# The head of an expert search: one half of the tokens first, and a shorter search for its first eight rows

## The chip, the cores and the metric

The kernel runs on one core of a Trainium2 chip. The metric is the device time of one execution in microseconds (us); less is better. The core has TensorE (PE), VectorE (DVE), ScalarE (ACT), GpSimd (POOL) and SyncE (SP, which here only issues DMAs), and 16 DMA engines that serve all queues.

## The reference, cut to what matters

Three model blocks run one after the other over 256 tokens of 1024 channels. The change lies where the second block ends and its expert layer (PEER) begins:

```python
def peer(h, wq, subkeys, u_tab, v_tab):
    q = (hf @ wq).reshape(T, PEER_HEADS, 2, PEER_DKEY // 2)          # 8 heads, two halves of 128
    sc = jnp.einsum('thpd,pnd->thpn', q, subkeys)                    # two lists of 128 scores
    top_v, top_i = lax.top_k(sc, PEER_TOPK)                          # 16 best of each list
    cand_v = top_v[:, :, 0, :, None] + top_v[:, :, 1, None, :]       # 256 sums of a pair
    best_v, best_j = lax.top_k(cand_v, PEER_TOPK)                    # the 16 best pairs
    ids = jnp.take_along_axis(cand_id, best_j, axis=-1)              # 16 rows of a table of 16384
    ...
```

`h` is the RMS-normed, modulated residual stream. Each token and head takes 16 rows `u`, `v` of the table; the layer's result is the sum over `gate * gelu(h . u) * v`. So 256 tokens x 8 heads x 16 rows are gathered.

## The kernel before

**Weights.** All weights come through one ring of five 512 KB slots: `_load` issues them on SP in a fixed order, each as soon as its slot is free. `_process` splits the next one into a high part (ACT, line 111) and a low part (DVE, line 115; GpSimd if asked); the slot is free when the low part is done. Three pairs of parts (`SPLIT`) can be held. `get` hands out the next pair and works ahead up to three. Each product is three matmuls (`mm3`: high x high, high x low, low x high). Every engine works off its instructions in the order in which the program writes them.

**End of the second block.** `x_add(g, r, p)` takes a product of 512 channels, scales it on DVE (line 976), adds it to `x` for each half `t` of the tokens (line 979; DVE for `g = 1, t = 1`, else GpSimd) and squares the result on ACT with a sum per token (line 237). `later` puts a call off, `settle` writes the calls that were put off.

**Head of `peer`.** The root of the sums of squares is taken for both halves at once (`rms_x`), both halves of `x` are scaled into `xn` (line 1071), the first two weights of `wq` are split (`ahead`, the second one's low part on GpSimd), and 16 transposes with their evictions give `hT` for 256 tokens. While TensorE has nothing to do, `keep_warm` writes idle transposes (line 278). Then, for head `r` = 0 and 1: `pair` makes the head's 48 matmuls of 256 columns, `half_scores` copies them to `q3` (line 1077), `half_products` multiplies by the subkeys (line 1084) and copies the scores to `sc` (line 1087), and `pump(99, r)` writes the whole search of the first 128 tokens for that head to DVE.

**The search** (`choose`) of one set `s` (128 tokens, one head) has 13 steps: the 8 best of 128, the next 8, for two lists (`top8`), 256 sums, the 16 best of them, and a decoding into row numbers `ids[s]` (line 1133) and gates. The table's rows are then gathered by GpSimd (line 1180), one indirect DMA per row `n` (128 tokens x 8 KB); set `s` is rows 16 s to 16 s + 15. Twelve places of 1 MB hold rows at first. `choice(n)` makes the dot product with row `n` (DVE, line 1206), the gate (ACT, lines 1215 to 1218) and the weighted sum (TensorE, line 1222), which frees the row's place. Beside the rows, every fourth `n` one more weight of `wq` is split and multiplied, and from `n = 16` one step of the search of set 2 is written behind most dots, so that the last step stands behind the dot of row 29.

Of the kernel before, what the change touches and what calls it, by code (L numbers as in the profile page):

```python
# [821 lines left out]
def block2(k, mod, M):  # L822
    nc, tc, a, x = k.nc, k.tc, k.a, k.x
# [21 lines left out]
    st = {}  # L845
# [184 lines left out]
def peer(k, mod, pA, normed_at):  # L1030
# [3 lines left out]
    nc, tc, a, x = k.nc, k.tc, k.a, k.x  # L1034
    tk = tc.alloc_tile_pool(name="tk", bufs=1, reuse_waits="tile")
# [4 lines left out]
    iota16 = tk.tile([128, 16], F32, name="iota16")  # L1040
# [22 lines left out]
    def halves(z):  # L1063
        return z.rearrange("p (s e) -> p s e", s=2)
# [1 line left out]
    topv, topi = [small(64 * i) for i in range(2)], [small(64 * i + 32, 32, U32) for i in range(2)]  # L1066
    bestv, besti = [small(128 + 32 * i, 16) for i in range(2)], [small(144 + 32 * i, 16, U32) for i in range(2)]
    topf, ji, jf, sel = small(192), small(224, 32, U32), small(256), small(288)
    r = k.rms_x(tk, "m2")
    for t in range(2):  # L1070
        nc.vector.tensor_scalar_mul(xn[:, t], x[:, t], r[:, t:t + 1])
    k.ahead(2)
    k.transposed(hT, xn, normed_at[0], normed_at[1], tmp=hfull, warm=40)
    nc.scalar.dma_start(subk, a["subk"])

    def half_scores(r, p):
        nc.scalar.activation(q3, p, AF.Copy)
        k.later(half_products, r)

    def half_products(r):  # L1080
        q, ps = q3, k.mm()
        for n in range(2):
            for t in range(2):
                nc.tensor.matmul(ps[:, t * 256 + n * 128:t * 256 + n * 128 + 128], q[:, n, t * 128:t * 128 + 128],
                                 subk[:, n * 128:n * 128 + 128], start=True, stop=True)
        for t in range(2):
            nc.scalar.activation(sc[t][:, 2 * r:2 * r + 2], ps[:, t * 256:t * 256 + 256], AF.Copy)

# [4 lines left out]
    def top8(v, i, src, n):  # L1093
        nc.vector.max(out=v[:, 8 * n:8 * n + 8], in_=src)
        nc.vector.max_index(out=i[:, 8 * n:8 * n + 8], in_max=v[:, 8 * n:8 * n + 8], in_values=src)
        if n == 0:
            nc.vector.match_replace(out=src, in_to_replace=v[:, 0:8], in_values=src, imm_value=-3.0e38)

    def choose(s):
        t, h = s // 8, s % 8  # L1100
        tv, ti, bv, bi = (z[s % 2] for z in (topv, topi, bestv, besti))
        st = {}

        def sums():
            nc.vector.tensor_tensor(cand.rearrange("p (a b) -> p a b", a=16),
                                    tv[:, 0:16].unsqueeze(2).to_broadcast([128, 16, 16]),
                                    tv[:, 16:32].unsqueeze(1).to_broadcast([128, 16, 16]), op=ALU.add)

        def gate():
            st["g"] = tk.tile([128, 16], F32, name="gate", bufs=6)  # L1110
            st["z"] = tk.tile([128, 2], F32, name="gz", bufs=2)
            nc.vector.tensor_scalar_mul(st["z"][:, 0:1], bv[:, 0:1], -1.0)
            nc.scalar.activation(st["g"], bv, AF.Exp, bias=st["z"][:, 0:1], accum_out=st["z"][:, 1:2])

        def decode():
            nc.vector.tensor_copy(topf, ti)
            nc.vector.tensor_scalar(ji[:, 0:16], bi, 4, None, op0=ALU.logical_shift_right)
            nc.vector.tensor_scalar(ji[:, 16:32], bi, 15, None, op0=ALU.bitwise_and)
            nc.vector.tensor_copy(jf, ji)

        def equal():
            nc.vector.tensor_tensor(eq, halves(jf).unsqueeze(3).to_broadcast([128, 2, 16, 16]),
                                    iota16.unsqueeze(1).unsqueeze(1).to_broadcast([128, 2, 16, 16]), op=ALU.is_equal)

        def pick():
            nc.vector.tensor_mul(eq, eq, halves(topf).unsqueeze(2).to_broadcast([128, 2, 16, 16]))

        def total():
            nc.vector.reduce_sum(halves(sel), eq, axis=AX.X)

        def rows():
            ids[s] = tk.tile([128, 16], I32, name="ids", bufs=6)
            nc.vector.scalar_tensor_tensor(ids[s], sel[:, 0:16], 128.0, sel[:, 16:32], op0=ALU.mult, op1=ALU.add)
# [6 lines left out]
        z = [lambda i=i, n=n: top8(tv[:, 16 * i:16 * i + 16], ti[:, 16 * i:16 * i + 16], sc[t][:, 2 * h + i], n)  # L1140
             for i in range(2) for n in range(2)]
# [26 lines left out]
    st = {"n": 0}  # L1168

    def refill():  # L1170
        while places and st["n"] < N and st["n"] // 16 in ids:
# [7 lines left out]
            i = ids[n // 16]  # L1179
            nc.gpsimd.indirect_dma_start(out=z, out_offset=None, in_=a["uv"],  # L1180
                                         in_offset=bass.IndirectOffsetOnAxis(ap=i[:, n % 16:n % 16 + 1], axis=0))
            st["n"] += 1

    def release(n):
# [8 lines left out]
    def tokens(t):  # L1193

        h2[0] = ps.tile([128, 1024], F32, name="h2")
        for c in range(8):
            nc.tensor.transpose(h2[0][:, c * 128:c * 128 + 128], hfull[:, c, t * 128:t * 128 + 128], k.ident)
# [56 lines left out]
    def rest():  # L1254
        for r in range(2, 8):
# [1074 lines left out]
```

## Time and profile before

| what | value |
| --- | --- |
| median of the runs (3) | 2525.92 us (2523.03 to 2526.9) |
| the profiled execution | 2522.51 us, its span 2520.6 us |
| granted TensorE clock, mean | 0.913 of full |
| DMA | 861.29 MB, mean 342 GB/s |
| busy: PE, DVE, ACT, POOL | 81%, 51%, 30%, 13% |

The profile is of one execution. The busy share of a span is a mean over stages with different limits: the stage that matters here runs from about 618 us (last products of the second block) over 669 us (first gather issued) to about 1380 us (last row used). "Idle before" in a row is the time that the engine stood still ahead of it, with the instruction that ended the wait.

### The profile page before, as it was taken

The page shows a single profiled execution, that of the slowest core. Times are in us where ns is not written, and L with a number is a line of the kernel's source. Part 1 is how long each engine was busy: PE and PEld are TensorE (multiplying, and loading weights), DVE is VectorE, ACT ScalarE, POOL GpSimd, SP SyncE. Part 2 cuts the span into 40 slices and gives each one's busy share as a digit, 9 for nine tenths or more (in the row PEclk, how much of TensorE's full clock was granted, in tenths as well). Part 3 has the DMA queues.
Part 4 walks back from the last instruction along what each step waited for, and adds up shares of the span by engine and source line. Part 5 has one row for each costly group of instructions (what it writes and reads, how often), then busy time and mean ns, then how long its engine had stood idle before and what let it go on. Part 6 is the DMA issues. An engine that isn't in the chain of part 4 may idle for free. (4 is left out here: it accounts for less than half of the span.)

```text
span 2520.6 us, 30184 instructions
## 1 busy us (share of the span) xinstructions
PE 2051.9 (81%) x11204; PEld 1195.5 (47%) x11204; DVE 1297.8 (51%) x2518; ACT 766.4 (30%) x1637; POOL 327.8 (13%) x315
## 2 busy tenths in 40 slices
PE   9899999899699888787886898966776676676766
PEld 8789898787555333343432897321221111121121
DVE  8987799877767687787855888100000000000001
ACT  5654444446344444454543443000000000000000
POOL 0100000000334333333341121000000000000000
PEclk9999999999899989899999999988778888888887
DMA  7767688775599999999998448999999999999997
GB/s 263 236 216 256 202 313 300 251 252 173 201 420 397 421 417 369 355 400 393 381 417 352 117 149 319 378 418 419 418 418 419 418 418 419 417 417 419 417 417 289
DMA packets 176307, 861.29 MB, mean 342 GB/s; under 512 B 29992, under 2 KB 35296, under 8 KB 107296
## 3 DMA queue, kind: packets, MB, share of 16 engines
q1 hardware_dynamic: 125872, 578.19, 59.9%
q0 software_dynamic: 36864, 268.45, 26.4%
q10 hardware_dynamic: 13424, 12.72, 1.7%
q8 instruction: 89, 1.46, 0.2%
q14 instruction: 58, 0.48, 0.1%
HBM read 858.19 MB, written 1.10 MB: 341 GB/s over the span
## 5 line engine op out<-in xcount | busy, mean ns | idle before, releaser
L115 DVE TENSOR_TENSOR wlo<-ring,whi 128x1024 fp32r<-128x1024 f32 x223 | 276.1, 1242 | 96.6 <-ACT whi L111 93.9
L1972 DVE TENSOR_TENSOR xe<-mm,m 128x256 f32<-128x256 f32 x15 | 6.4, 424 | 602.0 <-PE mm L1970 602.0
L111 ACT ACTIVATE whi<-ring 128x1024 fp32r<-128x1024 f32 x228 | 239.6, 1056 | 163.1 <-PE mm L162 40.3
L2014 PE MATMUL mm<-K,xe 128*32 128x512 f32 x864 | 147.1, 654 | 84.8 <-DMA K<-in_moe_w_dram 84.5
L2014 PE MATMUL mm<-we,xe 128*32 128x512 f32 x864 | 145.3, 765 | 84.1 <-DMA we<-in_moe_w_dram 83.7
L1222 PE MATMUL ys<-rowsS,diag 128*128 128x512 f32 x264 | 143.8, 685 | 53.6 <-ACT diag L1218 53.4
L161 PE MATMUL mm<-hTh,whi 128*128 128x256 f32 x608 | 172.4, 284 | 0.8 <-DVE hTl L309 0.8
L163 PE MATMUL mm<-hTh,wlo 128*128 128x256 f32 x608 | 169.6, 279 | 0.4 <-DVE wlo L115 0.4
L162 PE MATMUL mm<-hTl,whi 128*128 128x256 f32 x608 | 169.5, 279 | 0.0
L2035 ACT ACTIVATE he<-mm 128x512 f32<-128x512 f32 x16 | 9.5, 597 | 453.7 <-PE mm L2014 453.7
L1215 ACT ACTIVATE dots<-dots 128x1 f32<-128x1 f32 x256 | 51.5, 201 | 305.1 <-DVE rowsS L1206 84.0
L2117 POOL TENSOR_TENSOR x<-x,zT 128x512 f32<-128x512 f32 x1 | 1.6, 1560 | 962.1 <-ACT x L2116 962.1
L2051 ACT ACTIVATE heT<-mm 128x512 f32<-128x512 f32 x16 | 9.6, 597 | 378.8 <-PE mm L2049 368.5
L2014 PEld LDWEIGHTS mm<-K,xe 128*32 128x32 f32 x864 | 21.8, 112 | 208.4 <-DMA K<-in_moe_w_dram 196.2
L161 PEld LDWEIGHTS mm<-hTh,whi 128*128 128x128 f32 x608 | 115.1, 189 | 4.7 <-issue 2.5
L2081 DVE TENSOR_TENSOR ye<-mm,px_m 128x512 f32<-128x512 f32 x16 | 11.1, 692 | 206.4 <-PE mm L2075 206.4
L1222 PEld LDWEIGHTS ys<-rowsS,diag 128*128 128x128 f32 x264 | 53.8, 217 | 132.5 <-ACT diag L1218 81.5
L2014 PEld LDWEIGHTS mm<-we,xe 128*32 128x32 f32 x864 | 20.7, 119 | 201.5 <-DMA we<-in_moe_w_dram 183.5
L162 PEld LDWEIGHTS mm<-hTl,whi 128*128 128x128 f32 x608 | 115.5, 190 | 0.8
L163 PEld LDWEIGHTS mm<-hTh,wlo 128*128 128x128 f32 x608 | 114.9, 189 | 0.6 <-DVE wlo L115 0.6
L1222 PE MATMUL ys<-rowsL,diag 128*128 128x512 f32 x192 | 95.4, 631 | 23.7 <-ACT diag L1218 23.3
L375 DVE SCALAR_TENSOR_TENSOR mod<-ring,mod_t,mod 128x1024 f32<-128x1024 f32 x84 | 109.4, 1303 | 0.1
(528 smaller groups left out, 4801.8 us busy)
## 6 DMA issues: line engine op xcount, KB each, us to landing
we<-in_moe_w_dram SPq DMA_DIRECT2D x160, 1024.0 KB
K<-in_moe_w_dram SPq DMA_DIRECT2D x122, 1024.0 KB
ring<-in_moe_w_dram SPq DMA_DIRECT2D x100, 512.0 KB
K<-in_moe_w_dram SPq DMA_DIRECT2D x84, 512.0 KB
ring<-in_w_in_dram SPq DMA_DIRECT2D x48, 512.0 KB
ring<-in_ada_w_dram SPq DMA_DIRECT2D x48, 512.0 KB
ring<-in_mod_w_dram SPq DMA_DIRECT2D x48, 512.0 KB
ring<-in_w_qkv_dram SPq DMA_DIRECT2D x24, 512.0 KB
```

What stands on the lines that cost most here:

```text
L111: nc.scalar.activation(hi, raw, AF.Copy)
L115: (lower or nc.vector).tensor_sub(lo, raw, hi)
L161: nc.tensor.matmul(out, lhs[0], rhs[0], start=start, stop=False)
L162: nc.tensor.matmul(out, lhs[0], rhs[1], start=False, stop=False)
L163: nc.tensor.matmul(out, lhs[1], rhs[0], start=False, stop=stop)
L375: nc.vector.scalar_tensor_tensor(z, raw, th[:, ch:ch + 1], z, op0=ALU.mult, op1=ALU.add)
L1215: nc.scalar.activation(g, a, AF.Gelu)
L1222: nc.tensor.matmul(ys[-1][:, 512 * j:512 * j + 512], d, rows[n][1][:, 1024 + 512 * j:1536 + 512 * j], start=n % 128 == 0, stop=n % 128 == 127)
L2014: nc.tensor.matmul(p[32 * j:32 * j + 32], xe[:, c], w[j], start=c == 0, stop=c == 7)
L2035: nc.scalar.activation(he, hs[0], AF.Tanh, scale=0.5)
L2051: nc.scalar.activation(heT, p, AF.Copy)
L2081: nc.vector.tensor_mul(ye, p, m5)
```

## The change

The first 128 tokens (t = 0) go ahead of the second 128 through norm, transposes, head 0's products and scores. `quick` finds the first eight rows of set 0 from the 8 best of each list alone (64 sums), and these are gathered; the full search then finds the other eight. GpSimd and DVE swap the halves in `x_add`, the first `wq` weight is split ahead of the last `x_add`, and the second on DVE. `first` holds the first two split weights for both halves. `ids[s]` becomes a list of single columns, so that `refill` can issue rows 0 to 7 before 8 to 15 are known; for set 0 the first `top8` of each list shrinks to its `match_replace` (`without`), since `quick` has done the rest. Cut to its core:

```diff
-            (nc.vector if g and t else nc.gpsimd).tensor_add(xs, xs, y)
+            (nc.vector if g and not t else nc.gpsimd).tensor_add(xs, xs, y)
...
     k.rows_part(p3, yT, 3, 4)
+    k._process()
     k.later(x_add, 1, 1, p3)
...
-    r = k.rms_x(tk, "m2")
-    for t in range(2):
-        nc.vector.tensor_scalar_mul(xn[:, t], x[:, t], r[:, t:t + 1])
-    k.ahead(2)
-    k.transposed(hT, xn, normed_at[0], normed_at[1], tmp=hfull, warm=40)
     nc.scalar.dma_start(subk, a["subk"])
+    def norm_rows(t):
+        v = v2[:, t:t + 1]
+        nc.vector.tensor_add(v, k.ss[:, 0, t:t + 1], k.ss[:, 1, t:t + 1])
+        nc.vector.tensor_scalar(v, v, 1.0 / 1024, 1e-6, op0=ALU.mult, op1=ALU.add)
+        nc.vector.tensor_scalar_mul(xn[:, t], x[:, t], k.rsqrt(tk, v, 1, f"m2{t}"))
+    def transposed_rows(t, warm=0):
...
+        k.keep_warm(ps[0], warm)
+        for c in range(8):
+            nc.tensor.transpose(ps[c // 4][:, c % 4 * 128:c % 4 * 128 + 128], xn[:, t, c * 128:c * 128 + 128], k.ident)
+        def lower(q):
+            c4 = slice(4 * q, 4 * q + 4)
+            nc.vector.tensor_sub(hT[1][:, c4, u], hfull[:, c4, u], hT[0][:, c4, u])
+        for q in range(2):
...
+            nc.scalar.activation(hT[0][:, 4 * q:4 * q + 4, u], hfull[:, 4 * q:4 * q + 4, u], AF.Copy)
+            if q:
+                lower(0)
+        lower(1)
+    def cols_of_rows(w, t, out):
+        for c in range(8):
+            k.mm3(out, [z[:, c * 128:c * 128 + 128] for z in w], [z[:, c, t * 128:t * 128 + 128] for z in hT], c == 0,
+                  c == 7)
+    def first_scores(t):
+        u = slice(t * 128, t * 128 + 128)
+        p = k.mm()[:, 0:256].rearrange("p (n t) -> p n t", n=2)
+        for i in range(2):
+            cols_of_rows(first[i], t, p[:, i])
+        nc.scalar.activation(q3[:, :, u], p, AF.Copy)
+        half_products(0, (t,))
+    norm_rows(0)
+    transposed_rows(0, warm=44)
+    k._process()
+    norm_rows(1)
+    first = [k.parts.pop(0) for _ in range(2)]
+    first_scores(0)
+    transposed_rows(1)
...
+    def quick():
+        tv, ti, bv, bi = (z[0] for z in (topv, topi, bestv, besti))
+        for i in range(2):
+            src, u = sc[0][:, i], slice(16 * i, 16 * i + 8)
+            nc.vector.max(out=tv[:, u], in_=src)
+            nc.vector.max_index(out=ti[:, u], in_max=tv[:, u], in_values=src)
+        c, e8 = cand[:, 0:64], eq[:, :, 0:8, 0:8]
...
+        ids[0] = [ids8[:, e:e + 1] for e in range(8)]
...
-    for r in range(2):
-        k.later(half_scores, r, k.pair(hT))
-        k.settle()
-        if r == 0:
-            tokens(0)
-        k.settle()
-        pump(99, r)
-        refill()
+    quick()
+    refill()
+    tokens(0)
+    first_scores(1)
+    pump(99, 0)
+    refill()
+    k.later(half_scores, 1, k.pair(hT))
+    k.settle()
+    k.settle()
+    pump(99, 1)
+    refill()
```

## Rows read from the trace of the kernel before

**Rows 1.** The page: GB/s in 40 slices of the span; queue of the gathers.

```profile
GB/s 263 236 216 256 202 313 300 251 252 173 201 420 397 421 417 369 355 400 393 381 417 352 117 149 319 378 418 419 418 418 419 418 418 419 417 417 419 417 417 289
q0 software_dynamic: 36864, 268.45, 26.4%
```

**Rows 2.** Windows; columns: busy time per engine, granted clock, DMA share, GB/s.

```profile
652.00:653.00 1.00, 1.00 (x9) 1.00 (x8) 0.97 (x4) 1.00 (x5) 0.00 (x0) 0.82 0.01 4
669.00:671.00 2.00, 1.49 (x8) 1.19 (x8) 2.00 (x3) 0.47 (x2) 1.84 (x1) 0.60 0.00 0
671.00:672.00 1.00, 0.00 (x0) 0.00 (x0) 0.97 (x4) 0.18 (x1) 0.70 (x2) 0.50 0.83 94
682.00:720.00 38.00, 35.69 (x131) 20.21 (x132) 20.70 (x34) 16.80 (x49) 14.75 (x14) 0.94 1.01 420
760.00:762.00 2.00, 2.00 (x15) 1.52 (x14) 1.93 (x7) 1.22 (x5) 0.96 (x2) 1.00 0.30 123
```

**Rows 3.** Lines, VectorE, 660 to 760 us: busy, mean ns, idle before.

```profile
L1206 DVE SCALAR_TENSOR_TENSOR G<-G,h 128x1024 f32<-128x1024 f32 x19 | 23.0, 1215 | 9.5 <-DMA G<-in_uv_dram,ids 9.5
L1206 DVE SCALAR_TENSOR_TENSOR early<-early,h 128x1024 f32<-128x1024 f32 x11 | 13.1, 1214 | 4.7 <-DMA early<-in_uv_dram,ids 4.7
L115 DVE TENSOR_TENSOR wlo<-ring,whi 128x1024 fp32r<-128x1024 f32 x9 | 11.0, 1232 | 12.6 <-ACT whi L111 12.6
```

**Rows 4.** Timeline of GpSimd: issues of the gathers.

```profile
669.16 2.20 POOL L1180 DMA_INDIRECT early<-in_uv_dram,ids  x1 [23.16 <-DVE gz L1136]
671.66 0.95 POOL L1180 DMA_INDIRECT early<-in_uv_dram,ids  x1 [0.30 <-issue]
760.74 0.94 POOL L1180 DMA_INDIRECT G<-in_uv_dram,ids  x1 [16.71 <-DVE gate L1137]
```

**Rows 5.** Timeline of ScalarE and GpSimd at the end of the second block.

```profile
632.50 1.05 ACT L111 ACTIVATE whi<-ring 128x1024 fp32r<-128x1024 f32 x1
636.88 0.63 ACT L237 ACTIVATE junk<-x 128x512 f32<-128x512 f32 x1 [3.32 <-POOL x L979]
635.56 1.29 POOL L979 TENSOR_TENSOR x<-x,s 128x512 f32<-128x512 f32 x1 [1.89 <-DVE s L976]
```

**Rows 6.** Timeline of VectorE there and in the norm.

```profile
636.47 0.93 DVE L979 TENSOR_TENSOR x<-x,s 128x512 f32<-128x512 f32 x1
637.40 0.74 DVE L976 SCALAR_TENSOR_TENSOR s<-mm,rso,g 128x512 f32<-128x512 f32 x1
641.04 0.16 DVE L244 TENSOR_TENSOR vm<-ssf 128x2 f32<-128x2 f32 x1 [0.99 <-ACT junk L237]
643.05 3.50 DVE L1071 TENSOR_SCALAR early<-x,rsm 128x1024 f32<-128x1024 f32 x2
```

**Rows 7.** Timeline of TensorE: transposes, the products' first and last, a narrow one.

```profile
646.61 3.46 PE L296 MATMUL mm<-ident,early 128*128 128x128 f32 x15 [2.42 <-DVE early L1071]
649.78 0.58 PE L161 MATMUL mm<-hT3h,whi 128*128 128x256 f32 x1
657.04 0.28 PE L163 MATMUL mm<-hT3h,wlo 128*128 128x256 f32 x1
617.26 1.00 PE L906 MATMUL ac<-v,sT 128*128 128x64 f32 x8
```

**Rows 8.** Timeline of VectorE: search of head 0, first dot.

```profile
659.62 0.29 DVE L1094 MAX8 early<-early 128x8 f32<-128x128 f32 x1 [2.89 <-ACT early L1087]
666.51 0.69 DVE L1122 TENSOR_TENSOR early<-early,iota 128x512 f32<-128x512 f32 x1
668.69 0.18 DVE L1133 SCALAR_TENSOR_TENSOR ids<-early 128x16 int32<-128x16 f32 x1
680.91 1.21 DVE L1206 SCALAR_TENSOR_TENSOR early<-early,h 128x1024 f32<-128x1024 f32 x1
```

**Rows 9.** Timeline of SyncE: loads of wq.

```profile
655.25 1.83 SPq L96 DMA_DIRECT2D ring<-in_wq_dram  x2
670.36 0.33 SPq L96 DMA_DIRECT2D ring<-in_wq_dram  x1
```

More of the change, by code (lines that the diff above doesn't have):

```diff
@@ L1078, in half_scores, with half_products @@
         k.later(half_products, r)
-    def half_products(r):
+    def half_products(r, ts=(0, 1)):
         q, ps = q3, k.mm()
         for n in range(2):
-            for t in range(2):
+            for t in ts:
                 nc.tensor.matmul(ps[:, t * 256 + n * 128:t * 256 + n * 128 + 128], q[:, n, t * 128:t * 128 + 128],
                                  subk[:, n * 128:n * 128 + 128], start=True, stop=True)
-        for t in range(2):
+        for t in ts:
             nc.scalar.activation(sc[t][:, 2 * r:2 * r + 2], ps[:, t * 256:t * 256 + 256], AF.Copy)
+    def first_scores(t):
+        u = slice(t * 128, t * 128 + 128)
+        p = k.mm()[:, 0:256].rearrange("p (n t) -> p n t", n=2)
[10 more added lines that the diff above has]
+    transposed_rows(1)
     ids, gates = {}, {}
@@ L1096, in top8, with without @@
         if n == 0:
-            nc.vector.match_replace(out=src, in_to_replace=v[:, 0:8], in_values=src, imm_value=-3.0e38)
+            without(v, src)
+    def without(v, src):
+        nc.vector.match_replace(out=src, in_to_replace=v[:, 0:8], in_values=src, imm_value=-3.0e38)
+    def quick():
[5 more added lines that the diff above has]
+        c, e8 = cand[:, 0:64], eq[:, :, 0:8, 0:8]
+        nc.vector.tensor_tensor(c.rearrange("p (a b) -> p a b", a=8), tv[:, 0:8].unsqueeze(2).to_broadcast([128, 8, 8]),
+                                tv[:, 16:24].unsqueeze(1).to_broadcast([128, 8, 8]), op=ALU.add)
+        nc.vector.max(out=bv[:, 0:8], in_=c)
+        nc.vector.max_index(out=bi[:, 0:8], in_max=bv[:, 0:8], in_values=c)
+        nc.vector.tensor_scalar(ji[:, 0:8], bi[:, 0:8], 3, None, op0=ALU.logical_shift_right)
+        nc.vector.tensor_scalar(ji[:, 16:24], bi[:, 0:8], 7, None, op0=ALU.bitwise_and)
+        for i in range(2):
+            u = slice(16 * i, 16 * i + 8)
+            nc.vector.tensor_copy(topf[:, u], ti[:, u])
+            nc.vector.tensor_copy(jf[:, u], ji[:, u])
+        nc.vector.tensor_tensor(e8, halves(jf)[:, :, 0:8].unsqueeze(3).to_broadcast([128, 2, 8, 8]),
+                                iota16[:, 0:8].unsqueeze(1).unsqueeze(1).to_broadcast([128, 2, 8, 8]), op=ALU.is_equal)
+        nc.vector.tensor_mul(e8, e8, halves(topf)[:, :, 0:8].unsqueeze(2).to_broadcast([128, 2, 8, 8]))
+        nc.vector.reduce_sum(halves(sel)[:, :, 0:8], e8, axis=AX.X)
+        ids8 = tk.tile([128, 8], I32, name="ids8")
+        nc.vector.scalar_tensor_tensor(ids8, sel[:, 0:8], 128.0, sel[:, 16:24], op0=ALU.mult, op1=ALU.add)
+        ids[0] = [ids8[:, e:e + 1] for e in range(8)]
     def choose(s):
@@ L1131, in rows @@
         def rows():
-            ids[s] = tk.tile([128, 16], I32, name="ids", bufs=6)
-            nc.vector.scalar_tensor_tensor(ids[s], sel[:, 0:16], 128.0, sel[:, 16:32], op0=ALU.mult, op1=ALU.add)
+            z = tk.tile([128, 16], I32, name="ids", bufs=6)
+            nc.vector.scalar_tensor_tensor(z, sel[:, 0:16], 128.0, sel[:, 16:32], op0=ALU.mult, op1=ALU.add)
+            ids[s] = ids.get(s, []) + [z[:, e:e + 1] for e in range(len(ids.get(s, [])), 16)]
         def norm():
@@ L1138, in norm, with half @@
             gates[s] = st["g"]
-        z = [lambda i=i, n=n: top8(tv[:, 16 * i:16 * i + 16], ti[:, 16 * i:16 * i + 16], sc[t][:, 2 * h + i], n)
-             for i in range(2) for n in range(2)]
+        def half(i, n):
+            top8(tv[:, 16 * i:16 * i + 16], ti[:, 16 * i:16 * i + 16], sc[t][:, 2 * h + i], n)
+        z = [lambda i=i, n=n: half(i, n) for i in range(2) for n in range(2)]
+        if s == 0:
+            z[0::2] = [lambda i=i: without(tv[:, 16 * i:16 * i + 8], sc[0][:, i]) for i in range(2)]
         z += [sums] + [lambda n=n: top8(bv, bi, cand, n) for n in range(2)]
@@ L1170, in refill @@
     def refill():
-        while places and st["n"] < N and st["n"] // 16 in ids:
+        while places and st["n"] < N and st["n"] % 16 < len(ids.get(st["n"] // 16, ())):
             owner, z = places.pop(0)
@@ L1178, in refill @@
             use[owner] += 1
-            i = ids[n // 16]
+            i = ids[n // 16][n % 16]
             nc.gpsimd.indirect_dma_start(out=z, out_offset=None, in_=a["uv"],
-                                         in_offset=bass.IndirectOffsetOnAxis(ap=i[:, n % 16:n % 16 + 1], axis=0))
+                                         in_offset=bass.IndirectOffsetOnAxis(ap=i, axis=0))
             st["n"] += 1
```

9 lines of the change are left out of this document (added).

## The prediction

> **What bounds the kernel now.** I read the page first: the GB/s of the 40 slices sit near 400 from slice 12 on, so from about 690 to 1320 us and again from about 1560 to the end the kernel lives on its DMAs; the gathers' queue alone moves 268 MB, 256 rows of 1.05 MB [rows 1]. Then the windows: while the gathers run the DMA engines are full (share 1.01, 420 GB/s), so a row costs 2.5 us and a 512 KB weight 1.25 us; before the first gather they are idle (share 0.00 from 669 to 671 us, first bytes between 671 and 672) [rows 2]. So the first gather's moment sets, at first sight, all that follows: what comes behind the gathers is a chain that shifts with them.
>
> One more window spoils that: at 760 to 762 us the share drops to 0.30 [rows 2]. GpSimd's timeline says why: row 32, the first of set 2, is issued at 760.74 after 16.71 us in which GpSimd waited for DVE's last step of set 2's search [rows 4]. Check: data from 671.8, 32 rows at 2.5 us and the seven weights still to load at 1.25 us end at 671.8 + 80 + 8.75 = 760.55. The DMA engines had finished all they were given, and by the share (0.6 us busy of the two) stood still until row 32's bytes came, some 1.5 us. Row 32 is a gate: whatever the head gains must pass it. It opens when DVE has done 30 dots and the 13 steps of set 2.
>
> How much slack has DVE before that gate? First dot at 680.91 [rows 8], gate at 760.74: 79.8 us. In this time its 30 dots waited 9.5 + 4.7 = 14.2 us for rows to land [rows 3]; the other 65.6 us are its own work and its waits for the weights' high parts. So the gate opens either with the rows' landing, or 65.6 us after the first dot.
>
> **The change part by part.**
>
> *The split weight ahead of the last `x_add`.* DVE adds half 0 of the first `x_add` (started at 635.5 at once after scaling, 0.8 us), so that half 1's scaling ends near 637.0, GpSimd's addition (1.29 us) near 638.3 and its square on ACT near 639.05; only then may ACT take the high part (1.05 us, to 640.1) [rows 5, 6]. DVE's low part (1.24 us [rows 3]) stands ahead of the last `x_add` and waits for it: DVE goes on at 641.3, while before it scaled at 637.40 [rows 6]. This costs 3.9 us on the path. Then scaling 0.74, addition 0.8, square 0.75: half 0's sums at 643.7, against 641.04 for both halves [rows 6].
>
> *Norm of one half.* Before, 15 small instructions for two columns take 2.0 us (641.04 to 643.05) and two scalings 3.50 us, because the second shares its time with GpSimd's low part [rows 6]. One column's nine dependent instructions take at least 1.0 and at most 2.0; I take 1.75, and 0.82 for one scaling (the first transposes follow the first scaling by that). Half 0 is ready at 646.25; both halves were at 646.55 (transposes from 646.61 [rows 7]). Gain so far 0.35 us.
>
> *Transposes and products.* 15 transposes took 3.46 us, 0.22 each, the half clock; the clock rose between 652 and 653 (0.82 granted) [rows 2, 7]. Eight end at 648.3. Evictions of four 128-column pieces each on DVE and ACT, the wide high parts (about 0.6) and low parts (0.65) let the first products start at 649.0 and run from 649.65; the second group of channels is there at 651.0, the second weight at 652.6. The 48 products of 256 columns took 7.5 us before [rows 7]. Those of 128 columns are not in the trace. Lower bound: half, 0.058 us each at full clock; upper bound: as before, 0.117. The nearest row has even fewer columns, 64, a new weight for each, and still 0.105 us from start to start (8 in 1.00 us, the last one 0.27) [rows 7], so the weight load sets the pace; I take 0.11 at full and 0.22 at half clock. Twelve at half clock until the clock rises, 36 at 0.11: end at 656.4, against 657.32. Bounds: 654 (half price, clock up early) to 659 (clock at half throughout).
>
> By the Trainium skill, TensorE: Matmul & The Clock Gate, section LDWEIGHTS, a load of 128 columns takes 107 ns whatever is multiplied; the row agrees. Its section Back-to-back issue gap gives 81 ns for a pair at 128 columns; by it the 48 products would be some 1.4 us shorter, my third rival.
>
> *Scores.* A copy, two subkey products instead of eight, a copy: scores at 657.8, against 659.6 (search from 659.62 [rows 8]). Gain 1.8 us.
>
> *The other half's transposes, ahead of `quick` on DVE.* They stand behind the subkey products on TensorE, and their four evictions and two low parts stand before `quick` on DVE; the last waits for ACT's second high part, which waits for five pieces and the score copy. 3.4 us: `quick` starts at 661.2, 1.6 us later than the search did.
>
> *The short search.* Before, 659.62 to the row numbers' end at 668.87 are 9.25 us [rows 8]. `quick` has two `max` and `max_index` (1.2), 64 sums (0.25), one more pair (0.6), eight small decodings (0.75), and three operations on 128 instead of 512 elements (0.69 less 384 elements at about 1 ns, so 0.33 each), the numbers 0.2: 4.0 us. Row numbers at 665.2: 3.7 us earlier. The first issue took 2.20 us, others 0.95 [rows 4]; before, DVE ran two low parts beside it, now it would run searches. I count 1.25 less for it. Before, the first bytes were those of weights, at 671.8; after, rows' bytes follow the issue's end (666.4) by 0.5 us (as behind row 32) to 2; I take 668.2, as the first row's came late before. The stream starts 3.6 us earlier.
>
> *What the stream must carry.* SP loads a weight when a slot comes free, that is behind a low part. Before, two loads were issued at 655.25 and ran while the DMA engines were idle, the next at 670.36 [rows 9]. After, both first weights are held until head 0 is through, and the third's low part stands on DVE behind the full search of set 0 (its high part on ACT behind that search's gate): 674.5. So nine instead of seven weights load beside the rows: 2.5 us. The stream of the first 32 rows ends at 668.2 + 80 + 11.25 = 759.45, 1.1 us earlier, and rows land 1.1 us earlier.
>
> *Head 1.* On DVE: `quick` to 665.2, the rest of set 0's search 8.1 us to 673.3 (without two `max` and `max_index`), low parts to 676.9. TensorE had stood still (as before at 669 to 671: clock 0.60 [rows 2]), so its 48 products from 674.5 begin at half clock and end near 682.5; copy, subkey products, copies to 685.0; search of set 1 9.5 us: first dot at 694.5 instead of 680.91 [rows 8]. Of the 13.6 us, the 14.2 us in which dots waited for rows pay, just: 694.5 + 65.6 = 760.1, gate 0.6 us earlier than 760.74. The twelve places last until 668.2 + 30 + 5 = 703; row 0's place is free at about 697.5, so this gives no gap.
>
> **Sum.** The gate opens at the later of 759.65 (rows landing) and 760.1 (DVE's work): 0.6 us earlier. The extra products for the second half (48 more, 5.3 us) lie on TensorE's idle time beside DVE's searches, and the selected rows' work behind the gate is the same. The profiled execution: 2522.5 - 0.6 = 2521.9. The median of the runs shown is 3.4 us above it, so I give 2525.9 - 0.6 = 2525.3.
>
> **The rivals.**
>
> *Slower: the first dot comes too late.* Place: set 1's search on DVE, behind four low parts and TensorE's cold products. It decides from a first dot at 695.1 on; each us beyond that is a us. Speaks for it: my estimate is only 0.6 us below. With a first dot at 700 (clock at half throughout adds 3, low parts waiting for buffers 2) the time is 2530.8. Against: DVE's 65.6 us hold 12.6 us of waits for high parts [rows 3], some of which may shrink. Chance 0.23, in two thirds of it under 5 us.
>
> *Faster: the whole head passes.* If weights find gaps and the gate opens early, the stream's 3.6 us remain, and with products at half price and the full clock 2.5 more: 2522.3 to 2519.8. The gate's gap of 1.5 us speaks for it, the 1.01 share against [rows 2]. Chance 0.13.
>
> *Products shorter than the weight load allows in the row.* 1.4 us earlier all along: the gate 2 us earlier, 2523.9. Chance 0.14.
>
> *Forecast:* within 2 us of 2525.3. Chance 0.50.
>
> **How the numbers follow.** A median of three moves by some 2 us (2523.0 to 2526.9), so 0.2%, 5 us, is about what can be told from no change. Forecast and third rival lie within it; of the slower case a third and some unforeseen wait lie beyond, 0.15; of the faster case two thirds, 0.09. Same: 0.76. The range goes from the faster case's middle to the slower case's 700 us dot: 2520.5 to 2531; the forecast's own is 2523 to 2527.5.
>
> **What would show it.** Right: last `x_add` scaling near 641.3 behind a low part; first gather issued near 665.5; first dot near 694.5; hardly a wait of the first 25 dots for rows; row 32 issued near 760. Wrong: row 32 past 763 (late dots), or before 757; products of 128 columns at 0.06 us; the clock high through the transposes; a third wq pair of loads before the gathers.

## The result and the profile after

The changed kernel takes 2542.64 us (median of 4 runs, 2538.6 to 2544.79) where the kernel before takes 2525.36 (4 runs, 2523.03 to 2526.9): the ratio is 1.0078 [1.0061, 1.0094], 17 us slower. The forecast was 2525.3 and the range ended at 2531. The profiled execution has a span of 2542.5 us, before 2520.6; these two lie 22 us apart, the medians 17, so the traces below show somewhat more than the change costs in the median.

The timeline of VectorE after shows the head: start, duration, instruction, and in brackets the idle time before it with what ended it.

```profile
641.41 0.74 DVE L976 SCALAR_TENSOR_TENSOR s<-mm,rso,g 128x512 f32<-128x512 f32 x1
643.73 1.23 DVE L1075 TENSOR_TENSOR vm<-ssf 128x1 f32<-128x1 f32 x1 [0.19 <-ACT junk L237]
646.72 0.75 DVE L1077 TENSOR_SCALAR early<-x,rsm 128x1024 f32<-128x1024 f32 x1
652.70 0.69 DVE L1089 TENSOR_TENSOR hT3l<-early,hT3h 128x512 fp32r<-128x512 f32 x1 [0.59 <-ACT hT3h L1099]
670.13 0.29 DVE L1160 MAX8 early<-early 128x8 f32<-128x128 f32 x1
673.70 0.17 DVE L1178 SCALAR_TENSOR_TENSOR ids<-early 128x8 int32<-128x8 f32 x1
682.65 2.36 DVE L115 TENSOR_TENSOR wlo<-ring,whi 128x1024 fp32r<-128x1024 f32 x2 [0.51 <-ACT whi L111]
694.50 0.29 DVE L1146 MAX8 early<-early 128x8 f32<-128x128 f32 x1 [9.49 <-ACT early L1121]
703.99 1.21 DVE L1293 SCALAR_TENSOR_TENSOR early<-early,h 128x1024 f32<-128x1024 f32 x1
```

The last `x_add` scales at 641.41, as forecast. But `quick` starts only at 670.13, where the search before started at 659.62 [rows 8]; it lasts 4 us as forecast. The search of set 1 waits 9.49 us for its scores, and the first dot starts at 703.99, not 680.91 [rows 8].

GpSimd's timeline after holds the gathers of rows 0, 12, 30, 31, 32, 200 and 255:

```profile
674.16 1.15 POOL L1267 DMA_INDIRECT early<-in_uv_dram,ids  x1 [29.22 <-DVE early L1152]
...
710.32 0.94 POOL L1267 DMA_INDIRECT early<-in_uv_dram,ids  x1 [18.65 <-PE ys L1309]
...
753.64 0.94 POOL L1267 DMA_INDIRECT G<-in_uv_dram,ids  x1 [0.78 <-PE ys L1309]
755.35 0.94 POOL L1267 DMA_INDIRECT G<-in_uv_dram,ids  x1 [0.78 <-PE ys L1309]
779.31 0.94 POOL L1267 DMA_INDIRECT G<-in_uv_dram,ids  x1 [23.02 <-issue]
...
1236.85 0.94 POOL L1267 DMA_INDIRECT rowsL<-in_uv_dram,ids  x1 [2.05 <-PE ys L1309]
...
1392.98 0.94 POOL L1267 DMA_INDIRECT early<-in_uv_dram,ids  x1 [1.51 <-PE ys L1309]
```

The first gather comes 5.0 us later than before [rows 4], not 3.7 earlier. Row 12, the first that needs a place given back, waits 18.65 us for a product `ys`. Row 32 is 18.57 us behind its time before (760.74 [rows 4]); row 200 is 20.05 us behind and row 255 22.3 (before 1216.80 and 1370.68). In this trace what is lost by row 32 is not made up.

The windows after (busy time by engine, granted clock, DMA share, GB/s):

```profile
652.00:653.00 1.00, 0.83 (x4) 0.83 (x5) 0.41 (x2) 0.97 (x3) 0.00 (x0) 0.50 0.00 0
655.00:658.00 3.00, 3.00 (x16) 3.00 (x16) 2.17 (x9) 0.00 (x0) 0.00 (x0) 0.50 0.52 171
710.00:720.00 10.00, 10.00 (x42) 6.02 (x41) 8.06 (x11) 6.40 (x16) 4.54 (x4) 1.00 0.82 320
740.00:760.00 20.00, 20.00 (x89) 12.58 (x88) 13.51 (x36) 7.37 (x22) 7.18 (x8) 1.00 1.01 419
772.00:780.00 8.00, 8.00 (x37) 5.13 (x37) 5.61 (x12) 4.51 (x13) 0.69 (x1) 1.00 0.01 3
```

Three things are to be seen. At 652 to 653 the clock stands at half (0.50), where before it rose (0.82 [rows 2]), and stays there under the products. From 740 to 760 TensorE is busy for 20.00 of 20 us (17.95 before). And the gap ahead of row 32, some 1.5 us before [rows 2], is now longer than 7 us (share 0.01 from 772 to 780).

And VectorE's lines after, 670 to 780 us (busy, mean ns, idle before), beside [rows 3]:

```profile
L1293 DVE SCALAR_TENSOR_TENSOR G<-G,h 128x1024 f32<-128x1024 f32 x20 | 23.9, 1213 | 0.0
L115 DVE TENSOR_TENSOR wlo<-ring,whi 128x1024 fp32r<-128x1024 f32 x11 | 13.2, 1223 | 16.8 <-ACT whi L111 16.8
L1293 DVE SCALAR_TENSOR_TENSOR early<-early,h 128x1024 f32<-128x1024 f32 x11 | 13.0, 1214 | 0.0
```

The dots no longer wait for rows at all (14.2 us before), and yet row 32 comes 75.3 us behind the first dot, not 65.6.

### The profile page after: what moved, and what is told of

The parts are those of the page before. It is cut to its first block, busy times and chain, and to the rows that moved or that the text cites. A ratio compares the mean times of both kernels' runs of the same rounds, so it can differ in the third digit from the quotient of the medians.

```text
span 2542.5 us, 30308 instructions
## 1 busy us (share of the span) xinstructions
PE 2074.4 (82%) x11256; PEld 1225.9 (48%) x11256; DVE 1301.3 (51%) x2535; ACT 768.0 (30%) x1638; POOL 323.6 (13%) x314
```

## The experiments

Each ran beside the kernel before on the same chip; ratios are to before there. "Dot" is the start of the first dot, "row 32" the issue of its gather, both of the profiled execution. Kernels with the same head (before, e7, e12, e13, e17, e18) issue the first gather anywhere from 667.58 to 671.25, so moments of two traces compare to some 4 us only; distances within one trace, as from dot to row 32, hold better.

| kernel | first gather | dot | row 32 | ratio [95%] |
|---|---|---|---|---|
| before | 669.16 | 680.91 | 760.74 | 1 |
| after | 674.16 | 703.99 | 779.31 | 1.0078 [1.0061, 1.0094] |
| e1_gate | 674.62 | 704.46 | 766.77 | 1.0027 [1.0017, 1.0036] |
| e2_still | 675.12 | 704.89 | 780.30 | 1.0079 [1.0053, 1.0104] |
| e3_quick | 669.21 | 706.59 | 782.84 | 1.0086 [1.0062, 1.0110] |
| e4_warm | 669.17 | 698.78 | 773.99 | 1.0058 [1.0037, 1.0079] |
| e5_short | 664.74 | 684.38 | 759.12 | 0.9991 [0.9980, 1.0002] |
| e6_short_gate | 664.50 | 684.17 | 746.46 | 0.9930 [0.9917, 0.9944] |
| e7_gate_before | 667.58 | 679.33 | 746.78 | 0.9947 [0.9935, 0.9959] |
| e10_half_ys | 673.79 | 702.73 | 770.57 | 1.0034 [1.0022, 1.0046] |
| e12_late_dot | 667.60 | 702.49 | 777.61 | 1.0055 [1.0042, 1.0069] |
| e13_late_dot_gate | 670.47 | 705.45 | 767.35 | 1.0012 [1.0003, 1.0021] |
| e11_gate_half_ys | 672.72 | 702.54 | 757.64 | 0.9994 [0.9985, 1.0003] |
| e9_all | 662.38 | 700.46 | 762.49 | 1.0013 [1.0004, 1.0022] |
| e16_two_delays | 672.70 | 702.57 | 777.54 | 1.0066 [1.0053, 1.0079] |
| e15_set2_only | (no row of it is used) | | | 0.9990 [0.9981, 0.9998] |
| e17_free | 671.25 | 683.02 | 748.19 | 1.0088 [1.0072, 1.0104] |
| e18_free_late | 670.01 | 704.90 | 769.58 | 1.0161 [1.0145, 1.0178] |
| e19_free_after | 674.93 | 703.95 | 766.85 | 1.0170 [1.0151, 1.0188] |

**First: four edits of the changed kernel.** The theory was the "slower" rival of the prediction: the late first dot holds row 32 back, and the gate is the loss.

e1_gate, set 2's search two steps behind each of the first rows:

```
-            pump(1, min(ready, st["n"] // 16 + 3))
+            pump(2 if n < 32 else 1, min(ready, st["n"] // 16 + 3))
```

> The changed kernel, but up to row 32 two search steps instead of one are written behind each dot, so that set 2's search ends behind the dot of row 22 instead of row 29. Nothing is left out. Theory G (row 32 is a gate: the DMA engines run dry at 771 us because the gate opens at 779.3, and everything behind it keeps its distance): row 32 is issued near 768 to 771, the DMA engines no longer stand still between 771 and 780, and the time falls by 8 to 9 us, to about 2534. Theory S (the lateness comes from the first gather's issue, 5 us late, and the gap at row 12): neither moves, so no change, 2542 to 2543.

It gave back 0.51% (1.0078 to 1.0027), 13 us, more than expected. It looked like a confirmation; e7_gate_before below shows that it is none.

e2_still, in which `get` works ahead up to three weights again from the norm on:

```
+    k.still = False
     norm_rows(0)
```

> The changed kernel with the flag `still` set to False at the head of the expert layer, as the removed `ahead` did: `get` then works ahead up to three weights again. Theory G: head 1's products and the first dot stay (704 us, within 1), but the three low parts in a row at 710 to 714 become one, two of them moving into the 9.5 us in which DVE waited for head 1's scores: row 32 opens 3 to 4.5 us earlier, time 2538 to 2539.5. Theory S: first gather at 674.2 as before, no change.

Its part about the gate fell: two low parts moved ahead of the dot, so VectorE had 2.3 us less to do behind it, and row 32 came no earlier (75.4 us behind the dot); VectorE's waits for high parts grew by as much instead (18.7 us against 16.3). VectorE's own work is not what paces this stretch.

e3_quick, the second half's transposes behind `quick`:

```
     first_scores(0)
-    transposed_rows(1)
...
     quick()
     refill()
+    transposed_rows(1)
```

> The changed kernel with the second half's transposes written behind the short search instead of ahead of it. First gather at about 668.6 instead of 674.2, half a us ahead of the kernel before. Theory S: the time falls by that, 5 us, to 2537. Theory G: the second half's products, and with them head 1's and the first dot, come 0 to 4 us later (704 to 708), row 32 too, so the time is 2542 to 2546 in spite of the earlier gathers.

The first gather came 5 us earlier and nothing was won: dot and row 32 came 2.6 and 3.5 us later. The first gather's moment alone does not set the time of this kernel.

e4_warm, more warming products, and 24 more ahead of the first half's products:

```
-    transposed_rows(0, warm=44)
+    transposed_rows(0, warm=80)
...
+        k.keep_warm(p, 24 if t == 0 else 0)
```

> The changed kernel with 80 instead of 44 idle transposes ahead of the first transposes and 24 more between these and the first products, so that TensorE never stands still for long. Theory C (the products took 0.21 us each because the clock stood at half, and nothing in them lifts it): granted clock 1.0 up to the products, these 0.11 us each if the weight load sets the pace, 0.06 if the columns do, so scores 4 to 7 us earlier; if the clock stays up through the second half's products too, the first dot and row 32 come 7 to 12 us earlier, time 2530 to 2536. If the 128-column products let the clock fall again by themselves, less than 3 us. Rival (the clock does not matter, the low parts and copies pace the products): products keep 0.2 us or wait, no change or 1 us slower.

The windows of e4_warm:

```profile
653.00:658.00 5.00, 5.00 (x45) 5.00 (x46) 3.90 (x12) 1.38 (x2) 0.00 (x0) 1.00 0.28 75
664.00:668.00 4.00, 4.00 (x19) 4.00 (x20) 3.27 (x18) 0.49 (x1) 0.00 (x0) 0.50 0.00 0
```

With the clock kept up the first half's products run 45 in 5 us, 0.11 each: what products of 256 columns cost before. Halving the columns halves nothing. Weight loads fill the 5 us as products do (the second busy time in the row, 5.00 (x46)). Dot and row 32 both come 5.2 to 5.3 us earlier, between the two forecasts. The time falls by 0.2%, about as much, but the intervals of e4_warm and after overlap. The second half's products (664 to 668) are at half clock again.

**Second: the gate, the short search and TensorE, each by itself.** e5_short is the kernel before with `quick` and the row numbers as a list, called between the scores and `pump(99, 0)`, and no other part of the change; e6_short_gate adds e1_gate's edit to it; e7_gate_before is that edit alone in the kernel before.

> The kernel before with the short search of set 0 and nothing else of the change: head order, whole norm, 256-column products and the last x_add as before. Both theories: first gather near 664.2 instead of 669.16 (4 us of short search instead of 9.3). Pace theory (from the first dot to the gate at row 32 are 75.3 us, which TensorE's products of rows set, so that before had only 4.5 us to spare): the first dot comes some 2.6 us later (683.5), row 32 at 758.8 to 760, so at most 2 us of the 5 pass the gate: 2519.5 to 2522 where before gives 2521.7. Rival, my prediction's 65.6 us with 14.2 us to spare: the gate opens with the landing of the rows, row 32 at 755.5 to 757, time 2516.5 to 2518.

> As e5_short, and set 2's search takes two steps behind each of the first 32 rows instead of one. Gate theory: set 2's row numbers are there long before row 32 needs them, the stream's whole gain is kept: row 32 near 754 to 756, the hole in the DMA share behind 760 is gone, time 2515 to 2517.5. Rival, something behind the gate gives the gain back (places, the second half of the kernel): not better than the kernel before with the same two steps (e7_gate_before).

> The kernel before with two steps of set 2's search behind each of the first 32 rows. Gate theory: the gap at 760 to 762 (some 1.5 us of idle DMA engines) closes, row 32 at 758 to 759.5 instead of 760.74, time 2519.5 to 2520.5 where before gives 2521.7. Rival, the gap costs nothing (rows behind it are set by TensorE's pace alone): no change. Neither expects more than 2 us.

e5_short went as the pace theory said: 4.4 us earlier at row 0 (from the search's start to the first gather 4.05 us instead of 9.54), 1.6 at row 32, no difference that the runs can tell at the end. e7_gate_before missed both expectations: 0.53% (13 us) for a gap of 1.5 us. So e1_gate's 13 us are no sign that the gate makes the change's loss: the same edit gains as much where no dot is late. With the edit in both kernels the change still loses 0.8% (1.0027 against 0.9947), as without it. e6_short_gate, the short search without the new order of the head, is the fastest kernel of the study: 0.9930, 17 us under before, where 4 to 7 had been expected.

e10_half_ys is the changed kernel without the second product of rows 1 to 31 (half of these rows' part of the weighted sum is left out):

```
-        for j in range(2):
+        for j in range(1 if 0 < n < 32 else 2):
             nc.tensor.matmul(ys[-1][:, 512 * j:512 * j + 512], d, ...)
```

> The changed kernel, leaving out the second of the two products that weight and add a row, for rows 1 to 31 (so half of these rows' part of the sum is left out); nothing else differs. Theory that TensorE paces the stretch between the first dot and the gate: 0.86 us less of TensorE per row, so row 32 comes 66 to 70 us behind the first dot instead of 75.3, at 770 to 774, and the time falls by 5 to 9 us, to 2533 to 2537. Rival, DVE's dots, steps and low parts pace it (my prediction): nothing changes, 75 us, 2542.

Row 32 came 67.8 us behind the dot, the time fell by 0.44%, 11 us. TensorE's work paces the stretch in the changed kernel. The windows of e10_half_ys, the second from its first dot to row 32:

```profile
740.00:760.00 20.00, 14.97 (x72) 9.25 (x72) 16.42 (x42) 10.76 (x28) 4.68 (x5) 1.00 1.02 420
702.73:770.57 67.84, 55.79 (x244) 33.43 (x244) 53.80 (x107) 40.86 (x110) 20.75 (x21) 0.94 0.98 402
```

TensorE is busy for 14.97 of 20 us where after had 20.00. VectorE's 53.80 us of work, 13.0 of waits for high parts and 0.7 for rows now fill the 67.8 us, about the 65.6 that I had counted for it: they were the second limit, not the first. What the run does not show is how much of the 11 us belongs to the loss: the same products were never left out of the kernel before.

**Third: the late dot alone.** e12_late_dot is the kernel before with idle additions on VectorE; e13_late_dot_gate adds e1_gate's edit:

```
         pump(99, r)
+        for _ in range(32 if r else 0):
+            nc.vector.tensor_add(eq, eq, eq)
```

> The kernel before with 32 idle additions on DVE (0.72 us each) between set 1's search and the first dot; nothing else differs, the first gather, the weights' loads and the products stay. Theory that the first dot's moment alone makes the loss, because TensorE from then on needs 75 us to the gate: first dot near 704, row 32 near 779, time 17 to 20 us over before (2541 to 2544 where before gives 2524). My prediction's rule (65.6 us from the first dot, 14.2 to spare): row 32 near 769.6, 9 us over. Rival, the loss comes from the changed head's other parts (start of the stream, loads held back, clock): within 3 us of before.

> The same late first dot in e7_gate_before, so with two steps of set 2's search behind each of the first 32 rows. Gate theory (the loss is only the wait of row 32 for set 2's numbers): nothing of the delay is left, 2511 to 2514 as e7_gate_before. Backlog theory (TensorE works as long on a row as the DMA engines, so it never makes up a late first dot, and the gate is only where the DMA engines are seen idle): 15 to 19 us over e7_gate_before, 2526 to 2531.

The gathers of rows 12, 31 and 32 in e12_late_dot:

```profile
708.82 0.94 POOL L1180 DMA_INDIRECT early<-in_uv_dram,ids  x1 [22.87 <-PE ys L1222]
...
753.58 0.94 POOL L1180 DMA_INDIRECT G<-in_uv_dram,ids  x1 [0.78 <-DVE wlo L115]
777.61 0.94 POOL L1180 DMA_INDIRECT G<-in_uv_dram,ids  x1 [23.09 <-issue]
```

That is the picture of the changed kernel, from one delay. The ratio rose by 0.55%, 14 us (the median by 11), less than expected, and row 32 came at 777.61, not at the 769.6 of my prediction's rule. In e13_late_dot_gate the same delay costs 0.65% (1.0012 against 0.9947), 16 us. I took this as the end of the gate theory, too early: the timeline of VectorE in the two-step kernels shows set 2's row numbers at 745.84 in e7_gate_before and 766.41 in e13_late_dot_gate, and row 32 follows each within 1 us. Two steps moved the gate from 75 to 62 us behind the dot; they did not lift it. The last three runs try to.

e11_gate_half_ys is e1_gate with e10_half_ys's edit, leaving out the same products:

> e1_gate, leaving out the second of the two products that weight and add a row for rows 1 to 31 (half of these rows' part of the sum is left out), so 26 us less of TensorE's work and no gate. Backlog theory: TensorE makes the late first dot up, what is left is the stream's 5 us later start and the hole at 700 to 720 us: 2515 to 2521, 8 to 14 us under e1_gate. Rival, places (row 12 comes 20 us later because no place is free before, and this is never made up): 2526 to 2530, as e1_gate.

It gave 8 us (1.0027 to 0.9994), the least that the backlog theory expected. Some 0.47% over e7_gate_before are left: row 12 still comes at 708.86, as the places are given back no earlier. So less of TensorE's work does not give the whole loss back; what share of it is TensorE's stays unknown, since this edit too was not made in the kernel before.

e9_all joins e1_gate, e2_still, e3_quick and e4_warm:

> The changed kernel with all cures at once: two steps of set 2's search behind each of the first 32 rows, more warming products ahead of the first half's products, short search ahead of the second half's transposes, low parts of the third weight ahead of the norm. Backlog theory: the first gather comes near 664 to 666, but the first dot still near 697 to 702, so 12 to 17 us over e6_short_gate: 2519 to 2525, about as before. Start theory (the first gather's moment sets the end once the gate is lifted): 2508 to 2513, as e6_short_gate.

Its first gather is the earliest of all (662.38), and it is about as slow as e13_late_dot_gate, whose gather comes 8 us later. It is 21 us over e6_short_gate, where the backlog theory expected 12 to 17. The start theory falls again; the late dot at 700.46 is what the two have in common.

**Fourth: what was left over.** e16_two_delays has a filling and 7 of the idle additions ahead of set 0's search and 25 behind set 1's; e15_set2_only takes two steps only while set 2's search is open:

```
+            pump(2 if work and work[0][0] <= 2 else 1, min(ready, st["n"] // 16 + 3))
```

> The kernel before with two delays on DVE and nothing of the change: a filling and 7 idle additions (5.3 us) ahead of set 0's search, 25 more (18 us) behind set 1's. First gather near 674.5 and first dot near 704, as in the changed kernel. If the two moments make the whole loss: 15 to 19 us over before (ratio 1.006 to 1.0075), row 32 near 779. If the late start of the stream costs nothing beside the late dot: 10 to 12 us as e12_late_dot (1.0040 to 1.0050), and the rest of the change's loss lies in the weights' loads or the products.

> The kernel before with two steps behind a row only while set 2's search is not done; later sets keep their one step per row. If row 32's gate itself costs the 13 us: 2510 to 2514 (ratio 0.994 to 0.9955). If the gate costs only the gap seen in the DMA share and the rest of e7_gate_before's gain is the lead of the later sets: 2 to 4 us under before (0.9985 to 0.9992).

Two delays of idle work reproduce the change: row 32 at 777.54, span 2540.5 us, ratio 1.0066 [1.0053, 1.0079], whose interval overlaps the change's. Whether the later start of the stream adds to e12_late_dot's 1.0055 is not shown: those intervals overlap, and in the traces the two kernels are level up to row 80 (row 32 at 777.61 and 777.54, row 80 at 896.42 and 897.86) although their gathers start 5.1 us apart. They part between rows 80 and 128, where e12_late_dot's clock was granted in full (1.00 from 940 to 960 us) and e16_two_delays's was not (0.83 from 942 to 962). e15_set2_only gains 0.1%: row 32's gate alone is worth 2 to 3 us in the kernel before (by the interval, 0.5 to 5), near its gap of 1.5 us. By difference, the other 10 us or so of e7_gate_before come from the lead that the later sets' searches get.

**Last: row 32 free of set 2's search.** Set 2's scores are there after row 15, so five steps behind each row have its numbers ready after row 18, before a place is free for row 32. e17_free is this edit in the kernel before, e18_free_late with the late dot, e19_free_after in the changed kernel:

```
-            pump(1, min(ready, st["n"] // 16 + 3))
+            pump(5 if n < 128 else 1, min(ready, st["n"] // 16 + 3))
```

> The kernel before with five steps of the open set's search behind each of the first 128 rows, so that every set's numbers are there before a place is free for its first row. It is the base for the next two: 0.992 to 0.995 of before (two steps gave 0.9947). Row 32 no longer right behind set 2's numbers.

> e17_free with the late first dot of e12_late_dot (32 idle additions, 23 us), first gather as in the kernel before. Backlog theory (TensorE, once behind, never makes the dot up): 0.6 to 0.8% over e17_free, as e13_late_dot_gate over e7_gate_before. Gates theory (the lateness is carried on because each set's numbers hang on the rows done so far; without gates TensorE gains 1.5 us per four rows on the stream while weights are loaded): only the DMA engines' idle time around 705 us is lost, 5 to 8 us, 0.2 to 0.35% over e17_free.

> The changed kernel with the same five steps. Backlog theory: 0.7 to 0.9% over e17_free, about 1.000 to 1.002 of before. Gates theory: only the stream's 5 us later start and the idle 2 to 3 us around 710 us are lost, 7 to 9 us, 0.25 to 0.4% over e17_free, so 0.996 to 0.999 of before.

The base missed: e17_free is 0.9% slower than before, not 0.5 to 0.8% faster. Five steps in a row on VectorE hold back the dots behind them, TensorE stands still for want of them (busy 5.26 of 10 us):

```profile
730.00:740.00 10.00, 5.26 (x12) 1.73 (x10) 9.59 (x31) 4.76 (x10) 3.67 (x4) 1.00 1.02 423
```

But row 32 is free of set 2's numbers (738.71; the row comes at 748.19 and waits for a place). e18_free_late is 0.73% over e17_free, e19_free_after 0.82%, where the gates theory expected 0.2 to 0.4%. The first dot is 21.9 us later in e18_free_late than in e17_free, and so is the gather of row 255, at 1414.89 instead of 1392.98: the delay is carried through one to one. This does not clear the gates theory away, though, because the bursts of steps tie the rows to the search in another way. In e18_free_late the dots of rows 16 to 19 stand between them (750.25, 755.02, 758.03 for the last three), and rows 29 to 31 are issued only as the products of rows 17 to 19 give their places back:

```profile
754.78 1.13 POOL L1180 DMA_INDIRECT G<-in_uv_dram,ids  x1 [3.00 <-PE ys L1222]
760.01 0.94 POOL L1180 DMA_INDIRECT G<-in_uv_dram,ids  x1 [4.10 <-PE ys L1222]
764.35 0.94 POOL L1180 DMA_INDIRECT G<-in_uv_dram,ids  x1 [3.40 <-PE ys L1222]
```

In e17_free these three came 2.5 us apart (739.14, 741.63, 744.11). So the three runs show that the late dot is carried on without the wait for set 2's numbers, not that TensorE is what carries it.

## Why the prediction was wrong

The steps that held: the last `x_add` (641.3 forecast, 641.41 measured); `quick` at 4.0 us; the rest of set 0's search (8.1; 8.4); the way from `quick` to the first dot as a sum (33.3; 33.9), though head 1's products in it took 1.5 us longer and began 0.8 us sooner than its terms say; row 32 as the place where a late first dot is seen; 0.11 us for a product of 128 columns at full clock (e4_warm), against the rival that had it shorter.

**The step "`quick` starts at 661.2" failed by 8.9 us.** It went in four terms. The products were to start at 649.65 and, but for one, started from 652.17 on (2.5 us): I let the pieces on VectorE and ScalarE overlap, but they alternate (VectorE's wait 0.53 us for ScalarE's, ScalarE's 0.48 for VectorE's), and the norm took 3.0 us up to its scaling, above my bound of 2.0, since its first addition took 1.23 us beside GpSimd's. The products were to get the full clock after twelve of them. The order was the reverse: the clock was full through the first half's transposes (eight in 1.09 us), fell from 648 to 649 us (0.76) after TensorE had stood still for 4.14 us, and stayed at half through all 48 products, 0.21 us each, so that they ended at 662.4 instead of 656.4 (3.5 us beside the late start). The upper bound of 659 was too low by its own terms: 649.65 + 48 x 0.22 = 660.2. The copies and subkey products up to the scores took 2.1 us instead of 1.4. And the second half's transposes, evictions and low parts cost 5.5 us ahead of `quick` instead of 3.4, for the same alternation. With these the first dot, forecast at 694.5, came at 704.0; all but 0.6 us of the 9.5 are `quick`'s late start. e4_warm, with the clock kept up until the scores of the first half, gives 5.2 us back.

**The step "the gate opens 65.6 us after the first dot" failed by 9.7 us**, and with it the slack of 14.2 us and the bound of 695.1. I took all the time in which VectorE's dots waited for rows as time to spare, and did not ask which engine comes next when that wait goes; the sum has no term for TensorE between the first dot and the gate. It is TensorE. Two neighbouring places given back in the rows of after above are 1.72 us apart (753.64, 755.35): two f32 products of 512 columns. After every fourth row come 24 products of head 2 and on, as in TensorE's timeline of after:

```profile
732.83 1.88 PE L1309 MATMUL ys<-early,diag 128*128 128x512 f32 x4
734.14 0.68 PE L161 MATMUL mm<-hT3h,whi 128*128 128x256 f32 x1
734.66 0.28 PE L162 MATMUL mm<-hT3l,whi 128*128 128x256 f32 x1
...
737.42 4.03 PE L1309 MATMUL ys<-early,diag 128*128 128x512 f32 x9
```

The rows' products go on at 737.42, 2.9 us after the first of the 24 can have begun (the second follows at 734.66, 0.12 behind it). Four rows and such a group take 4 x 1.72 + 2.9 = 9.8 us; thirty rows and seven groups would be 71.9 us. The windows from the first dot to row 32, of after and of before, give nearly that:

```profile
703.99:779.31 75.32, 72.05 (x292) 43.22 (x293) 53.79 (x107) 40.85 (x110) 19.75 (x21) 0.96 0.88 361
680.91:760.74 79.83, 72.48 (x293) 42.48 (x294) 52.66 (x105) 38.81 (x108) 25.55 (x25) 0.97 1.01 418
```

TensorE has some 72 us of work in the stretch in both kernels (28 rows, almost seven groups, the subkey products). After, it stands still for 3.3 us of it, before for 7.4. How it holds a gate that VectorE opens is seen in what VectorE waited for meanwhile, after:

```profile
DVE wlo L115 <- ACT whi L111: 16.3, 7, 4.0
DVE early L1146 <- ACT early L1121: 4.8, 1, 4.8
```

Set 2's scores, which come off head 2's products, were 4.8 us late for VectorE, and the waits for high parts rose from 12.6 [rows 3] to 16.3 us; two of these high parts had waited for TensorE's products. With 1.1 us more of VectorE's own work that is the 9.7 us. In e10_half_ys the wait for the scores is gone and the other is 13.0 us. In the kernels other than before that keep one step behind a row and all products, the stretch is 74.7 to 76.3 us (after, e2_still, e3_quick, e4_warm, e5_short, e12_late_dot, e16_two_delays). Before had 79.8, so it had 4.5 us to spare, and by that a first dot was free until about 685.4; e5_short, with its dot at 684.38, lost nothing. 760.1 + 9.5 + 9.7 = 779.3 is where row 32 came.

**The rival was right in kind and wrong in size.** It priced a late dot up to row 32 alone, and took the gate for the cause. The late dot costs the same within the noise (some 0.13 to 0.23%) whatever the gate does: between kernels that differ by the delay alone 0.55% with the gate of before, 0.65% with the gate 13 us earlier, 0.73% with row 32 free of it; between the changed kernel and the one before 0.78, 0.80 and 0.82%. So the gate is where the DMA engines are seen idle for long, but moving it does not take the cost away.

What the loss is made of shows in the DMA engines' windows, of before and of after:

```profile
620.00:800.00 180.00, 151.12 (x704) 102.22 (x703) 128.87 (x310) 83.31 (x211) 59.61 (x55) 0.92 0.82 323
800.00:1100.00 300.00, 248.02 (x678) 114.43 (x676) 230.98 (x549) 136.71 (x389) 107.10 (x109) 0.92 0.98 389
620.00:800.00 180.00, 154.26 (x696) 111.28 (x695) 118.57 (x297) 73.98 (x183) 53.31 (x52) 0.85 0.71 279
800.00:1100.00 300.00, 244.82 (x690) 114.78 (x690) 229.27 (x546) 136.49 (x387) 100.35 (x103) 0.92 0.98 391
```

From 620 to 800 us they moved 58.1 MB before and 50.2 after. The 7.9 MB between them are 19 us at 420 GB/s, as much as row 32 is late (18.6). From 800 to 1100 us both kernels move the same at a share of 0.98, so there is hardly any idle time in which to catch up. Ahead of 800 us the engines run dry in two places: before row 12, which with twelve places can't be issued until the first dots are through, and at the gate. In after the first is short (share 0.63 from 710 to 715 us); in e12_late_dot, whose gathers start earlier, it is 0.01 from 705 to 710. How the loss divides between the later start, these two and TensorE's pace stays open: e10_half_ys and e11_gate_half_ys give back 8 to 11 us, without their like in the kernel before. After catches up 6 us between rows 12 and 28 (21.8 and 15.5 us behind before), and is thrown back at row 32; e18_free_late does the same against e17_free (20.6, 14.2, 21.4), there by the bursts of steps.

The part of the change that was to gain, the short search, does so: 4.4 us at the first gather in e5_short. In the median it was seen to pay only where the gate comes earlier and the head's order is left alone (e6_short_gate against e7_gate_before: 0.9930 against 0.9947, 4 us, with intervals that overlap a little).

## What to carry to other kernels

Where a wait is counted as slack, ask which engine would be next if it vanished, and add up that engine's whole work per step, f32 products at their measured distance; the slack is the difference of the two limits, not the wait. Splitting products by columns buys nothing where the weight loads already fill the time (0.11 us for 128 columns here, 0.12 for 256), and doubles their number. An edit that gives a loss back has to be made in the kernel before too: e1_gate looked like the proof of a theory that e7_gate_before then took away, and e10_half_ys, made in the changed kernel alone, can't say how much of its gain was the loss.

## What had not been expected of the hardware

- TensorE fed with products of 128 columns back to back, busy for 3.00 of 3 us, stayed at the lower clock level (0.50 granted) from 650 to beyond 662 us, and again through the second half's from 669 to 679 us, busy for 10.00 of 10 us. Under products of 256 columns, from 649.78 us on, the clock had risen at 652 to 653 in the kernel before [rows 2]; in after, under those of head 1 from 682.67 on, it rose only at 689 to 690 (0.76). With 36 more warming products ahead, and 24 in the gap, it stayed at the upper level through all 48.
- VectorE's addition of 128x1 elements took 1.23 us (643.73) while GpSimd's addition ran (643.68, 1.26 us); the second half's took 0.15 us (654.79) with GpSimd idle, and before it was 0.16 us for two columns [rows 6]. The Trainium skill, SBUF — State Buffer, section SBUF: two separate sides, says that the two engines share a port pair which one of them holds for its whole instruction, also where a VectorE operation with two inputs in SBUF meets a GpSimd operation that reads SBUF, as here; both ended within 0.02 us of each other, so the trace agrees.
